# A four-layer decoder trunk on one core: tail steps of the out projection given priority over weight splits, and keys split half by half on one engine, then on the other

## The chip, the cores and the metric

The kernel runs on one core of a Trainium2 chip. The metric is the device time of one execution in microseconds (us), lower is better. The core has a TensorE (PE in the profile, with its weight loads as PEld), a VectorE (DVE), a ScalarE (ACT), a GpSimd (POOL) and a SyncE (SP) that issues most DMAs here. Each engine takes its own instructions in the order in which the program puts them, and engines wait for one another through semaphores.

## The reference

The reference is a decoder trunk in float32: batch 1, 256 tokens, model width 1024, four layers. Each layer is `h = h + mixer(rms_norm(h))`, then `h = h + mlp(rms_norm(h))`.

```python
for i in range(4):
    a = rms_norm(h, attn_norm_g[i])
    y = [diff_attention, moba_attention, swa_sink_attention][i % 3](a, ...)   # 0, 1, 2, 0
    h = h + y
    a = rms_norm(h, mlp_norm_g[i])
    h = h + (jnp.maximum(a @ w_up, 0) ** 2) @ w_down      # 1024 -> 4096 -> 1024
return rms_norm(h, final_norm_g)
```

(The middle line is shortened here: the mixers take their own weights.) Layers 0 and 3 are differential attention (8 heads, two softmaxes of 64 wide queries and keys each, one subtracted from the other), layer 1 is block-sparse attention with 16 heads, which for 256 tokens is one block, layer 2 is sliding-window attention with 16 query heads, 2 key heads and sinks. All are causal and rotate the first quarter of each head. Every mixer ends in an out projection, 1024 by 1024, and it is the end of this projection, and the splitting of keys ahead of the scores, that the change concerns.

## The kernel before, in words

**Precision.** Every large product is made of split operands. A float32 value x is kept as a high part, rounded to the form fp32r that the matmuls take, and a low part, x minus the high part. A product is the sum of three matmuls: high by high, high by low, low by high. `mm3` (L269 to L273) issues the three; `block_step` (L604 to L606) does the same with two matmuls, one of 512 columns (weight high by both halves of the activation) and one of 256 (weight low by activation high).

**Weights.** All weights stream from memory in pieces of 1 MiB, 128 partitions by 2048. `fetch` puts a piece into one of four `raw` buffers by a DMA on SP (L66). `stage` (L68 to L82) splits it in two halves of 1024 columns: ACT copies to `whi` (L80), DVE subtracts to `wlo` (L81), into three buffers each. `take` (L86 to L93) hands the next split piece to its user, and before it does so it fetches up to five pieces ahead and splits up to two pieces ahead. So the instructions of a split stand in the program where a piece further back is taken, and in the program's order they stand ahead of the work on the piece that was just taken.

**Order.** The kernel is written in a language with a scheduler: it orders each engine's instructions by priority and by when it believes their inputs to be ready. Without anything said the priority is the order of the program. `tc.high_priority()` puts the instructions issued under it ahead of all others that could be scheduled at the same point. PE's instructions are scheduled in the same way, so their order also depends on when the scheduler believes their inputs to be there.

**The residual stream.** h is held transposed in four tiles `hT[j]` of 128 by 512; each holds two column blocks of the model width, so d = 0..7 counts the eight blocks of 128, each of 256 tokens. `into` (L614 to L626) adds one block of a projection's result: DVE adds it to hT (L624). Then `norm_part` (L222 to L229) makes the operand of the next projection: ACT writes the high part of h times the gain (`hg`, L228), DVE the low part (L229). After each second block `norm_sum` (L231 to L243) squares it on ACT (L233) and DVE adds up the squares (L238, L242). The scale of the norm itself is applied later.

**The out projection** of layers 0, 2 and 3 is `out_proj_all` (L629 to L644). It holds four PSUM banks, two blocks d in each. It takes four weight pieces (g = 0..3), and for each piece runs d = 0..7 with two `mm3` each (tile `p_d`). With the last piece, g = 3, each block is complete after its six matmuls, and `into(n, d, p, None, True)` follows at once (L644). The `take()` of g = 3 has just put the split of a piece two further on into the program. After the last block comes `up_proj`: 16 groups, each with a piece of weights and two banks `p_up`; the first group goes through k, the eight blocks of `hg`, in the outer loop, so its first matmul (L605) needs `hg` of block 0 alone. Layer 1 uses `out_proj`, which the diff doesn't touch.

**The keys.** The attention of layers 0, 1 and 3 goes through four groups of queries and keys each, layer 2 has one group of keys. DVE and ACT scale and rotate the projected q and k, PE transposes them (tile `p_qk`, L461), and `put_q` and `put_k` split the transposed tile out of PSUM. For keys the two heads of a pair are in partitions 0 to 63 and 64 to 127 of one PSUM bank, and `put_k` (L474 to L478) writes each into its own columns of `kpadh` (high, ACT, L477) and `kpadl` (low, DVE, L478); the rest of these tiles is zero. `scores` then calls `mm3`, for each of two blocks of queries: its first matmul (L271) and its third (L273) need `kpadh`, its second (L272) needs `kpadl` (tile `p_s`). Between the matmuls of the scores PE has those of the next input projection (tile `p_in`, L296).

Of the kernel before, what the change touches and what calls it, by code (L numbers as in the profile page):

```python
# [24 lines left out]
HD = 64  # L25
# [9 lines left out]
def f(ap):  # L35
    return ap.bitcast(F32)
# [3 lines left out]
def trunk(ctx: ExitStack, tc: tile.TileContext, xT, gains, lams, swa_row, fng, weights, out):  # L40
# [8 lines left out]
    def bank(tag, name):  # L49
        return ps.tile([P, 512], F32, tag=tag, name=name, bufs=4)  # L50
# [35 lines left out]
    def take():  # L86
        i = used[0]
        used[0] += 1
        while len(fetched) < min(weights.shape[0], i + FAR + 1):
            fetch()  # L90
        while len(staged) < min(weights.shape[0], i + LOOK + 1):
            stage()
        return staged[i]  # L93

    def r3(n):
        return lambda t: t.rearrange("p (a b) -> p a b", a=n)
# [120 lines left out]
    def new_norm(gain):  # L217
        n = Normed()
        n.gain, n.both, n.acc = gain, [], None
        return n  # L220

    def norm_part(n, d):  # L222

        j, b = d // 2, d % 2
        if b == 0:
            n.both.append(sb.tile([P, 2, 2, S], F32R, tag=f"hg{j}", name=f"hg{j}", bufs=1))
        both, h, g = n.both[j][:, b], hT[j][:, S * b:S * b + S], n.gain[:, d:d + 1]
        A.activation(both[:, 0], h, AF.Copy, scale=g)  # L228
        V.scalar_tensor_tensor(both[:, 1], h, g, f(both[:, 0]), op0=OP.mult, op1=OP.subtract)  # L229

    def norm_sum(n, j):  # L231
        sq = sb.tile([P, 512], F32, tag="relu", name="sq")
        A.activation(sq, hT[j], AF.Square)  # L233
        if j == 0:
            n.acc = sq
        else:
            acc = sb.tile([P, 512], F32, tag="u", name="acc2")
            V.tensor_tensor(acc, n.acc, sq, op=OP.add)  # L238
            n.acc = acc
        if j == 3:  # L240
            acc = sb.tile([P, S], F32, tag="rowx", name="acc3", bufs=1)
            V.tensor_tensor(acc, n.acc[:, :S], n.acc[:, S:], op=OP.add)  # L242
            n.acc = acc  # L243
# [25 lines left out]
    def mm3(out, lh, ll, rh, rl, start, stop, **kw):  # L269

        T.matmul(out, lh, rh, start=start, stop=False, **kw)  # L271
        T.matmul(out, lh, rl, start=False, stop=False, **kw)  # L272
        T.matmul(out, ll, rh, start=False, stop=stop, **kw)  # L273
# [198 lines left out]
        return q  # L472

    def put_k(k, p, n):  # L474
        for h in range(2):
            s = slice(HD * h, HD * h + HD)
            A.activation(k[0][s, :n, h, :], p[s], AF.Copy)  # L477
            V.tensor_tensor(k[1][s, :n, h, :], p[s], f(k[0][s, :n, h, :]), op=OP.subtract)  # L478

    def mixer_layer(i, n):  # L480
# [4 lines left out]
        if mixer == 2:  # L485
# [8 lines left out]
            for t in range(NT):  # L494
                V.scalar_tensor_tensor(kv[:, t, :], p[t], r[:, t:t + 1], rest[:, :256],
                                       op0=OP.mult, op1=OP.add)
            rope(kv[:, :, 0:P].rearrange("p t (s e) -> p t s e", e=HD), 2)
            put_k(kpad, turn(lambda b, t: kv[:, t, 0:P], 1), 1)
            kT = [x[:, 0] for x in kpad]
            first, second = [], []  # L500
# [26 lines left out]
        else:  # L527
# [4 lines left out]
            def QK(c):  # L532

                qs[c] = put_q(turn(lambda j, t: qk[c][:, t, P * j:P * j + P], 2))
                put_k(kpad, turn(lambda j, t: qk[c][:, t, P * (2 + j):P * (2 + j) + P], 2), 2)
# [72 lines left out]
    def joined(out, p):  # L608

        cross = sb.tile([P, S], F32, tag="cross", name="cross")  # L610
        A.activation(cross, p[:, S:], AF.Copy)  # L611
        V.tensor_tensor(out, p[:, :S], cross, op=OP.add)  # L612

    def into(n, d, p, row, whole=False):  # L614

        j, b = d // 2, d % 2
        h = hT[j][:, S * b:S * b + S]
        y = p
        if not whole:
            y = sb.tile([P, S], F32, tag="y", name="y")  # L620
            joined(y, p)
        if row is not None:
            V.tensor_tensor(y, y, row, op=OP.mult)
        V.tensor_tensor(h, y, h, op=OP.add)  # L624
        norm_part(n, d)
        if b:  # L626
            norm_sum(n, j)

    def out_proj_all(parts, n, rest):  # L629

        banks = [bank("acc", f"p_d{j}") for j in range(4)]
        for g in range(4):
            hi, lo = (r3(2)(x) for x in take())
            for d in range(8):
                if (g, d) == (2, 4):
                    rest()
                p = banks[d // 2][:, S * (d % 2):S * (d % 2) + S]
                w = slice(P * d, P * d + P)
                for a in range(2):
                    x = parts[2 * g + a]  # L640
                    mm3(p, hi[:, a, w], lo[:, a, w], x[:, 0], x[:, 1], g + a + d % 2 == 0, g + a == 4,
                        skip_group_check=True)
                if g == 3:
                    into(n, d, p, None, True)  # L644

    def out_proj(parts, n, rest):

# [134 lines left out]
    n = new_norm(gv[:, 0, 0, :])  # L782
# [5 lines left out]
    for i in range(DEPTH):  # L788
        parts, rest = mixer_layer(i, n)
        n = new_norm(gv[:, 1, i, :])  # L790
        (out_proj if i % 3 == 1 else out_proj_all)(parts, n, rest)
        held = {}

# [21 lines left out]
        if i + 1 < DEPTH:  # L815
            n = new_norm(gv[:, 0, i + 1, :])
# [81 lines left out]
```

## Time and profile before

| | |
|---|---|
| Time, median of 3 runs | 1148.51 us (1148.4 to 1148.52) |
| Time of the profiled execution | 1148.08 us |
| Its span in the profile | 1146.0 us |
| Granted TensorE clock, mean | 0.998 of full speed |
| PEld busy | 86% of the span |
| DVE busy | 72% |
| ACT busy | 58% |
| Memory traffic | 198.66 MB, mean 173 GB/s |

The span goes from the first to the last instruction that the profiler saw; the time of the execution has 2.08 us more around it. Rows of the timeline begin with the start and the duration in us, then engine, line, operation, what is written from what, and shape; several equal instructions in a row are drawn together (x2). In brackets stands how long the engine had been idle before, and what ended it. A row of the waits reads: who waited, for whom, us in total, times, longest. Ends of matmuls are modelled and overlap the next one's start.

### The profile page before, as it was taken

The page shows a single profiled execution, that of the slowest core. Times are in us where ns is not written, and L with a number is a line of the kernel's source. Part 1 is how long each engine was busy: PE and PEld are TensorE (multiplying, and loading weights), DVE is VectorE, ACT ScalarE, POOL GpSimd, SP SyncE. Part 2 cuts the span into 40 slices and gives each one's busy share as a digit, 9 for nine tenths or more (in the row PEclk, how much of TensorE's full clock was granted, in tenths as well). Part 3 has the DMA queues.
Part 4 walks back from the last instruction along what each step waited for, and adds up shares of the span by engine and source line. Part 5 has one row for each costly group of instructions (what it writes and reads, how often), then busy time and mean ns, then how long its engine had stood idle before and what let it go on. Part 6 is the DMA issues. An engine that isn't in the chain of part 4 may idle for free.

```text
span 1146.0 us, 17054 instructions
## 1 busy us (share of the span) xinstructions
PE 1135.6 (99%) x6560; PEld 988.2 (86%) x6560; DVE 827.8 (72%) x1608; ACT 660.0 (58%) x1207; POOL 11.4 (1%) x39
## 2 busy tenths in 40 slices
PE   9999999999999999999999999999999999999997
PEld 7789888888887888888899898888888889888886
DVE  8978977656676698766569887775567788777454
ACT  6866656544476675554446756554447676665342
POOL 1000000000000000000000000000000000000000
PEclk9999999999999999999999999999999999999999
DMA  8543465555543355555563346555554444554551
GB/s 330 195 147 119 167 198 193 198 194 184 184 147 133 125 184 188 190 203 191 185 208 111 111 148 214 190 184 185 187 195 136 148 143 160 191 198 169 184 184 37
DMA packets 30609, 198.66 MB, mean 173 GB/s; under 512 B 3521, under 2 KB 5185, under 8 KB 7361
## 3 DMA queue, kind: packets, MB, share of 16 engines
q1 hardware_dynamic: 30240, 197.06, 50.2%
q8 instruction: 51, 0.84, 0.3%
q10 hardware_dynamic: 288, 0.52, 0.1%
q14 instruction: 30, 0.24, 0.1%
HBM read 196.52 MB, written 1.05 MB: 172 GB/s over the span
## 4 chain that ended last, share of the span: by engine, by line
PE 95%; DVE 2%; DMA 1%; ACT 1%; issue 0%; SPq 0%; DVEq 0%; ACTq 0%
PE p_up L605 20%; PE p_in L296 18%; PE p_down L605 15%; PE p_up L606 11%; PE p_down L606 8%; PE p_last L272 3%; PE p_last L271 3%; PE p_last L273 3%; PE p_d L272 2%; PE p_d L273 2%; PE p_d L271 2%; DMA raw<-in_weights 1%; PE p_t L354 1%; PE p_s L271 1%; PE p_qk L461 1%; PE p_av L436 1%
## 5 line engine op out<-in xcount | busy, mean ns | idle before, releaser
L81 DVE TENSOR_TENSOR wlo<-raw,whi 128x1024 fp32r<-128x1024 f32 (+1 forms) x374 | 447.2, 1209 | 204.1 <-ACT whi L80 203.3
L80 ACT ACTIVATE whi<-raw 128x1024 fp32r<-128x1024 f32 (+1 forms) x374 | 384.3, 1046 | 216.4 <-issue 111.1
L605 PE MATMUL p_up<-hg,whi 128*128 128x512 f32 x1024 | 356.7, 393 | 0.5 <-DVE hg L229 0.2
L606 PE MATMUL p_up<-hg,wlo 128*128 128x256 f32 x1024 | 285.5, 280 | 0.0
L605 PE MATMUL p_down<-uu,whi 128*128 128x512 f32 x768 | 266.4, 391 | 0.0
L605 PEld LDWEIGHTS p_up<-hg,whi 128*128 128x128 f32 x1024 | 191.4, 187 | 42.8 <-DVE hg L229 0.7
L606 PE MATMUL p_down<-uu,wlo 128*128 128x256 f32 x768 | 215.0, 280 | 0.0
L296 PE MATMUL p_in<-whi,hg 128*128 128x512 f32 (+1 forms) x736 | 211.6, 371 | 0.0
L606 PEld LDWEIGHTS p_up<-hg,wlo 128*128 128x128 f32 x1024 | 193.5, 189 | 0.5
L605 PEld LDWEIGHTS p_down<-uu,whi 128*128 128x128 f32 x768 | 143.6, 187 | 31.5
L296 PEld LDWEIGHTS p_in<-whi,hg 128*128 128x128 f32 x736 | 132.2, 189 | 23.3 <-DVE hg L229 0.8
L606 PEld LDWEIGHTS p_down<-uu,wlo 128*128 128x128 f32 x768 | 145.2, 189 | 0.0
L296 PE MATMUL p_in<-wlo,hg 128*128 128x512 f32 (+1 forms) x368 | 130.4, 369 | 0.1
L680 ACT ACTIVATE uu<-u 128x512 fp32r<-128x512 f32 x64 | 40.5, 633 | 71.1 <-DVE u L678 71.1
L296 PEld LDWEIGHTS p_in<-wlo,hg 128*128 128x128 f32 x368 | 68.8, 189 | 12.3 <-DVE wlo L81 1.4
L611 ACT ACTIVATE cross<-p_up 128x256 f32<-128x256 f32 x128 | 47.9, 374 | 39.3 <-PE p_up L606 33.8
L228 ACT ACTIVATE hg<-hT,gn 128x256 fp32r<-128x256 f32 x64 | 31.6, 502 | 65.5 <-DVE hT L624 65.3
L339 ACT ACTIVATE e<-ns,nm 128x128 f32<-128x128 f32 (+1 forms) x128 | 56.8, 446 | 11.6 <-DVE nm L336 11.2
L681 DVE TENSOR_TENSOR uu<-u,uu 128x512 fp32r<-128x512 f32 x64 | 44.2, 691 | 21.4 <-ACT uu L680 21.4
L272 PE MATMUL p_d<-oo,whi 128*128 128x256 f32 x192 | 55.3, 288 | 0.0
L271 PE MATMUL p_d<-oo,whi 128*128 128x256 f32 x192 | 55.2, 288 | 0.0
L612 DVE TENSOR_TENSOR relu<-p_up,cross 128x256 f32<-128x256 f32 x128 | 53.6, 419 | 1.5 <-ACT cross L611 1.5
(182 smaller groups left out, 1247.2 us busy)
## 6 DMA issues: line engine op xcount, KB each, us to landing
raw<-in_weights SPq DMA_DIRECT2D x181, 1024.0 KB, 4.9
raw<-in_weights SPq DMA_DIRECT2D x8, 256.0 KB, 4.6
raw<-in_weights SPq DMA_DIRECT2D x4, 512.0 KB, 6.8
hT<-in_xT SPq DMA_DIRECT2D x8, 128.0 KB, 4.4
bias<-in_swa_row SPq DMA_DIRECT2D x1, 512.0 KB, 4.6
grow<-in_fng SPq DMA_DIRECT2D x1, 512.0 KB, 3.7
out<-res SPq DMA_DIRECT2D x4, 128.0 KB, 2.1
out<-res ACTq DMA_DIRECT2D x2, 256.0 KB, 2.2
```

The lines of the kernel that those rows point to most:

```text
L80: A.activation(hi[:, s], raw[:, s], AF.Copy)
L81: V.tensor_tensor(lo[:, s], raw[:, s], f(hi[:, s]), op=OP.subtract)
L271: T.matmul(out, lh, rh, start=start, stop=False, **kw)
L272: T.matmul(out, lh, rl, start=False, stop=False, **kw)
L273: T.matmul(out, ll, rh, start=False, stop=stop, **kw)
L296: T.matmul(out[t], n.both[k // 2][:, k % 2, x, P * t:P * t + P], r3(kb)(parts[k // kb][w])[:, k % kb, :], start=fresh, stop=k == 7 and x + ...
L339: A.activation(e[:, s], ns[:, s], AF.Exp, bias=nm[:, t:t + 1], scale=-1.0, accum_out=l[:, t:t + 1])
L605: T.matmul(r3(2)(p), hi, x, start=start, stop=False, skip_group_check=True)
L606: T.matmul(p[:, :S], lo, x[:, 0], start=False, stop=stop, skip_group_check=True)
L611: A.activation(cross, p[:, S:], AF.Copy)
L612: V.tensor_tensor(out, p[:, :S], cross, op=OP.add)
L681: V.tensor_tensor(both[:, :, 1], r3(2)(u), f(both[:, :, 0]), op=OP.subtract)
```

## The change

Two edits. `put_k` runs its two ACT copies first and then its two DVE subtractions, where it alternated between the engines before. In `out_proj_all` the call of `into` for a finished block is put under `tc.high_priority()`, so that its steps (L624, L228, L229, L233, L238, L242) are scheduled ahead of the weight splits (L80, L81) that stand before them in the program. Both kernels have the same instructions on every engine; their order differs on PE, DVE and ACT. On SP and POOL it is the same. After the change lines 479 to 643 have numbers higher by one, and later ones by two.

```diff
     def put_k(k, p, n):
-        for h in range(2):
-            s = slice(HD * h, HD * h + HD)
+        rows = [slice(HD * h, HD * h + HD) for h in range(2)]
+        for h, s in enumerate(rows):
             A.activation(k[0][s, :n, h, :], p[s], AF.Copy)
+        for h, s in enumerate(rows):
             V.tensor_tensor(k[1][s, :n, h, :], p[s], f(k[0][s, :n, h, :]), op=OP.subtract)
...
                 if g == 3:
-                    into(n, d, p, None, True)
+                    with tc.high_priority():
+                        into(n, d, p, None, True)
```

## The prediction

> **What bounds the kernel now.** I read the head of the page first, then the chain that ended last, then PE's own row of the waits, and only then the timelines of the places that the diff touches.
>
> ```profile
> span 1146.0 us, 17054 instructions
> ...
> PE 1135.6 (99%) x6560; PEld 988.2 (86%) x6560; DVE 827.8 (72%) x1608; ACT 660.0 (58%) x1207; POOL 11.4 (1%) x39
> ...
> PE 95%; DVE 2%; DMA 1%; ACT 1%; issue 0%; SPq 0%; DVEq 0%; ACTq 0%
> ```
>
> PE is busy 99% of the span and 95% of the chain. A kernel like this can only become faster where PE stands still. The view of waits gives all of these places:
>
> ```profile
> PE p_warm L133 <- POOL ones L124: 1.0, 1, 1.0
> PE p_qk L461 <- DVE qk L309: 0.7, 1, 0.7
> PE p_s L271 <- issue: 0.6, 1, 0.6
> PE p_up L605 <- DVE hg L229: 0.2, 1, 0.2
> ```
>
> That is 2.5 us, and only the last two lines touch the diff. The ends of matmuls are modelled, though, so a short stall hides inside a longer "busy" matmul. I therefore measure stalls by the distance from one start to the next. Nothing in the diff adds or removes an instruction; the same instructions stand in another order on PE, DVE and ACT, and SP's queue keeps its order. So the whole effect is stalls of PE that go or come.
>
> **Part 1, the end of the out projection (layers 0, 2 and 3; layer 1 uses another function).** In layer 0, DVE does this:
>
> ```profile
> 116.10 0.42 DVE L624 TENSOR_TENSOR hT<-p_d,hT 128x256 f32<-128x256 f32 x1 [2.12 <-PE p_d L273]
> 116.44 2.35 DVE L81 TENSOR_TENSOR wlo<-raw,whi 128x1024 fp32r<-128x1024 f32 x2
> 118.71 0.48 DVE L229 SCALAR_TENSOR_TENSOR hg<-hT,gn,hg 128x256 fp32r<-128x256 f32 x1
> 119.11 1.08 DVE L624 TENSOR_TENSOR hT<-p_d,hT 128x256 f32<-128x256 f32 x3
> ```
> ```profile
> 117.17 0.49 ACT L228 ACTIVATE hg<-hT,gn 128x256 fp32r<-128x256 f32 x1
> ```
> ```profile
> 118.83 0.28 PE L273 MATMUL p_d<-oo,wlo 128*128 128x256 f32 x1
> 119.25 0.50 PE L605 MATMUL p_up<-hg,whi 128*128 128x512 f32 x1
> 119.58 0.28 PE L606 MATMUL p_up<-hg,wlo 128*128 128x256 f32 x1
> 119.70 0.39 PE L605 MATMUL p_up<-hg,whi 128*128 128x512 f32 x1
> 119.93 0.28 PE L606 MATMUL p_up<-hg,wlo 128*128 128x256 f32 x1
> ```
>
> The high half of hg for block 0 is ready at 117.66, but its low half waits behind two weight splits (2.35 us) until 118.71. It ends at 119.19, and the up projection starts at 119.25. A 256-column matmul is followed after 0.12 us (119.58 to 119.70), a 512-column one after 0.23 (119.70 to 119.93). So 119.25 - 118.83 - 0.12 = 0.30 is lost, and 119.58 - 119.25 - 0.23 = 0.10 more behind it: 0.40 us. The other two layers show the same picture:
>
> ```profile
> 666.61 0.28 PE L273 MATMUL p_d<-oo,wlo 128*128 128x256 f32 x1
> 667.11 0.47 PE L605 MATMUL p_up<-hg,whi 128*128 128x512 f32 x1 [0.22 <-DVE hg L229]
> 667.41 0.28 PE L606 MATMUL p_up<-hg,wlo 128*128 128x256 f32 x1
> ```
> ```profile
> 957.72 0.28 PE L273 MATMUL p_d<-oo,wlo 128*128 128x256 f32 x1
> 958.12 0.50 PE L605 MATMUL p_up<-hg,whi 128*128 128x512 f32 x1
> 958.46 0.28 PE L606 MATMUL p_up<-hg,wlo 128*128 128x256 f32 x1
> ```
>
> Layer 2 loses 0.38 + 0.07, layer 3 loses 0.28 + 0.11. Together with layer 0 this is 0.40 + 0.45 + 0.39 = **1.24 us**, which is all that the first edit can win here.
>
> Does it win it? In the order of the changed kernel DVE does hT of block 0, only the first half of that split, and then hT and hg of the blocks as they come; the second half waits until nearly all blocks are through. By the durations above (1.18 for half the split, 0.33 from one hT to the next, 0.40 for an hg), hT of blocks 1, 2 and 4 are done at 118.6 and the hg of blocks 0 and 1 at 119.25 and 119.65. PE, in turn, has 18 matmuls of other blocks put ahead of p_up, so p_up comes at about 120.27, 0.6 us after its inputs. I take the whole 1.24 as gained. The bounds are 0 (another step of the row ends late in its place) and 1.24; the margin of 0.6 us puts it near the upper end.
>
> What is late next is the postponed second half of the split. DVE has the same work in the same stretch, so it does this one at about 124.2 to 125.4 instead of 117.6 to 118.8. PE needs it at step 4 of the second up group: from 120.27, sixteen steps of 0.12 + 0.23 = 0.35 us, six matmuls of the last block (0.7) and four more steps make 128.0. It has 2.6 us in hand. The raw buffer that it frees goes to a load on SP's queue:
>
> ```profile
> 118.82 0.33 SPq L66 DMA_DIRECT2D raw<-in_weights  x1
> ```
> ```profile
> raw<-in_weights SPq DMA_DIRECT2D x181, 1024.0 KB, 4.9
> ```
> ```profile
> 138.79 1.06 ACT L80 ACTIVATE whi<-raw 128x1024 fp32r<-128x1024 f32 x1 [1.33 <-PE p_up L605]
> ```
>
> The load is issued at 118.82, as the pair of splits ends. In the changed kernel it goes out at about 125.4 and lands 4.9 us later, at 130.3, and ACT reads that piece at 138.79. Nothing waits for it on SP but later loads of the same kind. I cost the postponed split at nothing; DVE's slack covers it, and without that cover each layer would pay up to the half split, 1.2 us.
>
> **Part 2, the keys.** Before, ACT splits keys of half 0, DVE subtracts them, then ACT does half 1:
>
> ```profile
> 317.95 0.58 ACT L477 ACTIVATE kpadh<-p_qk 64x512 fp32r<-64x512 f32 x1
> 319.41 0.59 ACT L477 ACTIVATE kpadh<-p_qk 64x512 fp32r<-64x512 f32 x1 [0.88 <-DVE kpadl L478]
> ```
> ```profile
> 318.70 0.67 DVE L478 TENSOR_TENSOR kpadl<-p_qk,kpadh 64x512 fp32r<-64x512 f32 x1
> ```
> ```profile
>   DVE kpadl L478: 8.5, 11
> ```
>
> The second ACT step starts 0.04 us after DVE's ends (318.70 + 0.67 = 319.37); the view of line 477 counts 11 such waits, 8.5 us on ACT. Both read the same PSUM bank, and the program has them take turns. Page "PSUM — Partial Sum Buffer" of the Trainium skill, section "PSUM bank collisions raise a hardware error", says that two engines may use one bank at once if their partition quadrants differ; the halves here lie in different quadrants. No run here shows such an overlap: by that rule the turns are the program's alone and new places for the instructions would gain nothing in the keys, which makes the sum of part 1 alone, 1147.3. In the changed order ACT does both halves in a row, without a wait for DVE, and half 1 ends about 1 us earlier (317.95 + 0.48 + 0.59 = 319.0 against 320.0). ACT's 8.5 us are themselves worth nothing, since ACT is 58% busy. What counts is when PE's first score matmul can start:
>
> ```profile
> 34.50 0.61 PE L296 MATMUL p_in<-whi,hg 128*128 128x512 f32 x2
> 35.72 0.59 PE L271 MATMUL p_s<-kpadh,qhl 128*128 128x256 f32 x2 [0.60 <-issue]
> ```
> ```profile
> 319.84 0.39 PE L296 MATMUL p_in<-wlo,hg 128*128 128x512 f32 x1
> 320.15 0.59 PE L271 MATMUL p_s<-kpadh,qhl 128*128 128x256 f32 x2
> ```
> ```profile
> 32.52 0.59 ACT L477 ACTIVATE kpadh<-p_qk 64x512 fp32r<-64x512 f32 x1
> 32.99 2.01 ACT L80 ACTIVATE whi<-raw 128x1024 fp32r<-128x1024 f32 x2
> 35.03 0.59 ACT L477 ACTIVATE kpadh<-p_qk 64x512 fp32r<-64x512 f32 x1
> ```
>
> At 35.72 PE has stood still for 35.72 - 34.50 - 2 x 0.23 = 0.76 us: two weight splits lie between the two key steps. That is the one large stall. At 320.15 it is 320.15 - 319.84 - 0.23 = 0.08. But the scheduler, which sees the keys ready earlier, also moves the first score matmuls ahead of 4 to 10 others in PE's order, at 11 places. In layer 0 they move ahead of 8 p_in: PE is there at 34.96 - 8 x 0.23 = 33.12, the keys are there at 32.52 + 0.48 + 0.59 = 33.59 and 0.10 later a matmul can start (as at 35.62 to 35.72), so PE waits 0.57 and gains 0.19. At 320.15 they move ahead of 5: arrival 318.92, keys 319.02 + 0.10, a wait of 0.20, so 0.12 is lost. The other places lie between no wait at all and a loss like this one. I take a loss of 0.05 at each of the ten, 0.5 us; the ends are a gain of 0.08 each (every wait goes, -0.8) and a loss of 0.2 each (+2.0).
>
> **The sum.** -1.24 - 0.19 + 0.5 = -0.9 us. The profiled execution took 1148.08 for a span of 1146.0, 2.08 outside it. After: span 1145.1, execution 1147.2. The median of the runs before is 1148.51, 0.43 above the profiled one, so the forecast is 1148.51 - 0.9 = **1147.6**. With the ends of the keys, and with 0 to 1.24 for the tails, this case alone reaches from 1146.3 to 1150.3 by its extremes, and I hold 1147.0 to 1148.2 for its core. A measurement of this kernel can tell about 0.2%, 2.3 us, from no change, so this counts as the same.
>
> **Rivals.**
> - *Every touched stall goes*: tails 1.24, the whole 0.76, and the waits of about 0.08 at ten places, 0.8: -2.8, 1145.7. For it: the keys are indeed ready 1 us earlier. Against it: the matmuls move by about as much.
> - *The score waits eat the tails' gain*: a loss of 0.13 at 11 places is 1.4, and the time is 1148.5. For it: the 0.12 worked out at 318.92.
> - *Slower, by the scores.* PE takes its matmuls in order, so a score matmul that is placed too early holds all the p_in behind it, as the 0.60 at 35.72 shows. (Page "TensorE: Matmul & The Clock Gate" of the Trainium skill, section on the 64-deep queue and the weight pull-ahead, says the same; this row agrees.) If half 1 of the keys isn't earlier, since ACT comes late to the pair, PE waits the whole moved distance, 4 x 0.23 = 0.92 or more. It decides from a mean loss of 1.43 / 11 = 0.13 us a place, and at 0.4 a place the time is 1148.51 - 1.43 + 4.4 = 1151.5. Against it: the ACT row at 317.95 starts on time now.
> - *The postponed split starves the up projection*: 1.2 us in three layers, 3.6 less the 1.4 gained, 1150.7. Against it: 2.6 us in hand.
> - *The change doesn't do what it says*: the scheduler leaves the splits where they are, and the first half of the split does stay ahead of hg. Then only the keys change: 1148.8.
>
> **Chances.** Forecast 0.48; every stall goes 0.14; waits eat the gain 0.16; slower by scores 0.10; starved 0.07; not done 0.05. Faster by over 0.2% (under 1146.2): most of the first rival and none of the forecast, 0.12. Slower by over 0.2% (over 1150.8): the slower half of the two slow rivals and what I have overlooked, 0.11. The same: 0.77. The range leaves out about 0.08 below and 0.10 above: 1146.0 to 1150.4.
>
> **What would show it.** Right: p_up starts 0.12 us after the last p_d ahead of it at all three tails; the second ACT key step follows the first without a wait for DVE; the first score of layer 0 has its wait cut from 0.76 to some 0.6. Wrong: PE waits for wlo in the second up group; waits of p_s on ACT kpadh that sum to over 2 us; a PE busy sum that differs from 1135.6 for a reason other than stalls.

## The result and the profile after

| Kernel | Median | Runs | Against before |
|---|---|---|---|
| before | 1148.51 us | 8 | |
| after | 1152.02 us | 8 (1151.35 to 1152.43) | 1.0029 (95%: 1.0020 to 1.0038) |

The change makes the kernel slower by 3.5 us, 0.3%. The forecast was 1147.6 us, and the time is above the upper end of the range, 1150.4. The profiled execution of after took 1152.43 us for a span of 1150.5, so the two profiles lie 4.5 us apart where the medians lie 3.5 apart.

The head of the page and the chain of after:

```profile
span 1150.5 us, 17080 instructions
...
PE 1138.9 (99%) x6560; PEld 987.9 (86%) x6560; DVE 828.3 (72%) x1608; ACT 660.6 (57%) x1207; POOL 11.4 (1%) x39
...
PE 94%; ACT 3%; DMA 1%; DVE 1%; issue 0%; SPq 0%; DVEq 0%; ACTq 0%
```

The numbers of matmuls and of DVE and ACT instructions are the same as before; the 26 instructions more in the first line are waits for semaphores, which don't count as busy. PE is busy 3.3 us longer with the same matmuls, and ACT has 3% of the chain where it had 1%. The view of PE's waits (who, for whom, us in total, times, longest) says where ACT came in:

```profile
PE p_s L271 <- ACT kpadh L477: 1.1, 6, 0.2
PE p_warm L133 <- POOL ones L124: 1.0, 1, 1.0
PE p_qk L461 <- DVE qk L309: 0.6, 1, 0.6
PE p_in L296 <- DVE wlo L81: 0.5, 1, 0.5
PE p_s L271 <- issue: 0.5, 1, 0.5
```

The first line is new: six first score matmuls wait for the ACT half of the key split. The wait of the up projection for `hg`, 0.2 us before, is gone. The same two things appear in the timelines.

**The tails.** DVE in layer 0 of after has one half of the split ahead of the `hg` steps, and the other behind them:

```profile
117.66 1.22 DVE L81 TENSOR_TENSOR wlo<-raw,whi 128x1024 fp32r<-128x1024 f32 x1
118.81 1.26 DVE L625 TENSOR_TENSOR hT<-p_d,hT 128x256 f32<-128x256 f32 x3
119.99 0.87 DVE L229 SCALAR_TENSOR_TENSOR hg<-hT,gn,hg 128x256 fp32r<-128x256 f32 x2
...
125.36 1.22 DVE L81 TENSOR_TENSOR wlo<-raw,whi 128x1024 fp32r<-128x1024 f32 x1
```

PE at the tails of layers 2 and 3 of after:

```profile
670.66 0.28 PE L273 MATMUL p_d<-oo,wlo 128*128 128x256 f32 x1
670.78 0.40 PE L606 MATMUL p_up<-hg,whi 128*128 128x512 f32 x1
671.01 0.28 PE L607 MATMUL p_up<-hg,wlo 128*128 128x256 f32 x1
```
```profile
962.41 0.28 PE L273 MATMUL p_d<-oo,wlo 128*128 128x256 f32 x1
962.53 0.40 PE L606 MATMUL p_up<-hg,whi 128*128 128x512 f32 x1
962.77 0.28 PE L607 MATMUL p_up<-hg,wlo 128*128 128x256 f32 x1
```

The up projection starts 0.12 us after the last out projection matmul ahead of it, where it started 0.50 and 0.40 after it before, and its second matmul follows 0.23 and 0.24 later. Layer 0 shows the same:

```profile
121.49 0.28 PE L273 MATMUL p_d<-oo,wlo 128*128 128x256 f32 x1
121.61 0.40 PE L606 MATMUL p_up<-hg,whi 128*128 128x512 f32 x1
```

The stalls of the tails are gone.

**The keys.** ACT and PE at the first keys of layer 1 of after:

```profile
318.86 1.20 ACT L477 ACTIVATE kpadh<-p_qk 64x512 fp32r<-64x512 f32 x2
```
```profile
319.63 0.40 PE L296 MATMUL p_in<-whi,hg 128*128 128x512 f32 x1
320.21 0.58 PE L271 MATMUL p_s<-kpadh,qhl 128*128 128x256 f32 x2 [0.18 <-ACT kpadh L477]
```

ACT doesn't wait for DVE between its two copies any more. But PE comes to the first score at 319.63 + 0.23 = 319.86 and starts it at 320.21: it stands still for 0.35 us where it lost 0.08 before. (The view of waits shows only 0.18 of it, since the matmul ahead is drawn as busy until 320.03.)

**The last up projection.** The matmuls of layer 3's up projection from 985 to 1045 us, grouped by line, before and then after (the columns are count, busy us and mean ns):

```profile
L605 PE MATMUL p_up<-hg,whi 128*128 128x512 f32 x174 | 60.4, 391 | 0.0
```
```profile
L606 PE MATMUL p_up<-hg,whi 128*128 128x512 f32 x171 | 60.5, 399 | 0.0
```

In 60 us PE starts 171 matmuls of 512 columns instead of 174, without any wait. At one place of both timelines, for two pairs of matmuls:

```profile
1000.12 0.39 PE L605 MATMUL p_up<-hg,whi 128*128 128x512 f32 x1
1000.36 0.28 PE L606 MATMUL p_up<-hg,wlo 128*128 128x256 f32 x1
1000.47 0.39 PE L605 MATMUL p_up<-hg,whi 128*128 128x512 f32 x1
1000.70 0.28 PE L606 MATMUL p_up<-hg,wlo 128*128 128x256 f32 x1
1000.82 0.39 PE L605 MATMUL p_up<-hg,whi 128*128 128x512 f32 x1
```
```profile
1000.08 0.40 PE L606 MATMUL p_up<-hg,whi 128*128 128x512 f32 x1
1000.32 0.28 PE L607 MATMUL p_up<-hg,wlo 128*128 128x256 f32 x1
1000.43 0.40 PE L606 MATMUL p_up<-hg,whi 128*128 128x512 f32 x1
1000.66 0.28 PE L607 MATMUL p_up<-hg,wlo 128*128 128x256 f32 x1
1000.78 0.40 PE L606 MATMUL p_up<-hg,whi 128*128 128x512 f32 x1
1001.02 0.28 PE L607 MATMUL p_up<-hg,wlo 128*128 128x256 f32 x1
1001.14 0.40 PE L606 MATMUL p_up<-hg,whi 128*128 128x512 f32 x1
```

Before, a pair takes 0.35 us each time. After, three pairs take 1001.14 - 1000.08 = 1.06, which is 0.353 each. Three matmuls fewer of 174, 1.7%, make 1.5 us over the 87 us that this goes on. **This was not in the prediction at all.**

**The start.** One part of the 4.5 us is seen in this execution alone: at 18.09 in after, and at 18.11 in a second profile of the same kernel.

```profile
18.09 0.73 PE L296 MATMUL p_in<-whi,hg 128*128 128x512 f32 x2
19.35 0.50 PE L296 MATMUL p_in<-wlo,hg 128*128 128x512 f32 x1 [0.53 <-DVE wlo L81]
```
```profile
18.11 0.63 PE L296 MATMUL p_in<-whi,hg 128*128 128x512 f32 x2
18.73 0.51 PE L296 MATMUL p_in<-wlo,hg 128*128 128x512 f32 x1
```

At 19.9 after is 0.76 us behind before, the second profile at the same matmul only 0.14. So this is a difference between executions, and may account for some of the gap between 4.5 and 3.5.

### The profile page after: what moved, and what is told of

Same layout as the page of the kernel before. It is cut to its first block, busy times and chain, and to the rows that moved or that the text cites. A ratio compares the mean times of both kernels' runs of the same rounds, so it can differ in the third digit from the quotient of the medians.

```text
span 1150.5 us, 17080 instructions
## 1 busy us (share of the span) xinstructions
PE 1138.9 (99%) x6560; PEld 987.9 (86%) x6560; DVE 828.3 (72%) x1608; ACT 660.6 (57%) x1207; POOL 11.4 (1%) x39
## 4 chain that ended last, share of the span: by engine, by line
PE 94%; ACT 3%; DMA 1%; DVE 1%; issue 0%; SPq 0%; DVEq 0%; ACTq 0%
PE p_up L606 21%; PE p_in L296 17%; PE p_down L606 15%; PE p_up L607 11%; PE p_down L607 8%; PE p_last L273 3%; PE p_last L272 3%; PE p_last L271 3%; PE p_d L271 2%; PE p_d L272 2%; PE p_d L273 2%; PE p_s L271 1%; PE p_t L354 1%; PE p_av L436 1%; DMA raw<-in_weights 1%; PE p_s L272 1%
## 5 line engine op out<-in xcount | busy, mean ns | idle before, releaser
L81 DVE TENSOR_TENSOR wlo<-raw,whi 128x1024 fp32r<-128x1024 f32 (+1 forms) x374 | 447.0, 1209 | 212.2 <-ACT whi L80 211.0
L80 ACT ACTIVATE whi<-raw 128x1024 fp32r<-128x1024 f32 (+1 forms) x374 | 384.1, 1045 | 215.2 <-issue 111.1
L339 ACT ACTIVATE e<-ns,nm 128x256 f32<-128x256 f32 (+1 forms) x128 | 56.8, 446 | 27.4 <-DVE nm L336 27.2
L228 ACT ACTIVATE hg<-hT,gn 128x256 fp32r<-128x256 f32 x64 | 31.4, 503 | 61.2 <-DVE hT L625 61.2
L273 PE MATMUL p_d<-oo,wlo 128*128 128x256 f32 x192 | 53.8, 284 | 0.0
```

Of the source, the lines that this page charges most:

```text
L80: A.activation(hi[:, s], raw[:, s], AF.Copy)
L81: V.tensor_tensor(lo[:, s], raw[:, s], f(hi[:, s]), op=OP.subtract)
L339: A.activation(e[:, s], ns[:, s], AF.Exp, bias=nm[:, t:t + 1], scale=-1.0, accum_out=l[:, t:t + 1])
```

## The experiments

Two theories at first. **A**: the keys cost the time, since the score matmuls move further forward than the keys do. **B**: the tail's priority does, by what it postpones. The first three kernels take the change apart.

**Keys alone.** The diff of `put_k` only.

> Only the key split of the change; the tail as before. Theory A (score matmuls moved ahead of keys that are not much earlier): in the changed kernel PE stands still some 0.3 us at each of about ten first scores where it stood 0.1 before, 2.0 us in all, so 1148.5 + 2.0 = 1150.5 here, or up to 1153.2 if the slower cadence of the last up projection and the longer start come with the keys. Theory B (the tail's priority starves or disturbs the up projections): 1148.5 to 1149.0 here.

Measured: 1151.59 us, ratio 1.0028 (1.0017 to 1.0038), against 1148.57 for before, measured beside it. +3.0 us, so the keys carry nearly all of the loss. The last up projection runs as before, 175 matmuls in those 60 us, so its slower cadence does not come with the keys.

**Tail alone.** The diff of `out_proj_all` only.

> Only the priority at the end of the out projection; keys as before. Theory A: the 1.24 us of the three tails are won, 1147.3. Theory B: slower than before, about 1151, with the up projection of layer 3 at 236 ns between matmuls of 512 columns where it had 230.

Measured: 1148.76 us, ratio 1.0003 (0.9994 to 1.0013). Neither theory has it: the gain of 1.24 doesn't show, and neither does a loss of 2.5. The stalls of the three tails are gone here too, and layer 3 has the slow cadence:

```profile
L605 PE MATMUL p_up<-hg,whi 128*128 128x512 f32 x171 | 60.5, 399 | 0.0
```

**Keys with later scores.** The key split, and the priority of the scores lowered by 28 places of the program's order:

```diff
+        at = tc.cur_priority
+        tc.cur_priority = at + 28
         for p, t, n in ((p0, 0, P), (p1, 1, S)):
             ...
             mm3(o, qh[:, a], ql[:, a], kh[:, :, :n], kl[:, :, :n], True, True)
+        tc.cur_priority = at + 6
```

In PE's order the first score then stands at, or within two matmuls of, its old place in eight of the twelve cases of layers 0, 1 and 3.

> The key split of the change, and the score matmuls given a later place in the program's priority, so that at eight of the eleven places PE's first score stands where it stood before. Theory A: the waits at these eight places go, about 8 x 0.28 = 2.2 us less than the key split alone, so 1148.3 to 1149. Theory B, and any theory in which the keys harm by something else: no different from the key split alone.

Measured: 1149.15 us, ratio 1.0005 (0.9996 to 1.0014), just over the 1149 of theory A. The key split is the same, ACT's two copies still stand in a row, and 2.4 of the 3.0 us are gone. At the first keys of layer 1 PE no longer waits:

```profile
320.15 0.39 PE L296 MATMUL p_in<-wlo,hg 128*128 128x512 f32 x1
320.37 0.28 PE L271 MATMUL p_s<-kpadh,qhl 128*128 128x256 f32 x1
```

So most of the harm is done by the place of the scores in PE's order, not by the key split as such: theory A holds for the keys. 0.6 us stays that the first scores don't explain.

**After, once more.** A second profile of the changed kernel.

> The changed kernel once more, for a second profile. If the longer start (0.76 us by 19.9) and the slower cadence in the up projection of layer 3 (236 ns, 1.7 us) belong to the kernel, both are there again; if they are chance, one or both are gone, and the rest (score waits of about 0.35 us, tails shorter by 0.4) stays.

Measured: 1151.88 us, span 1149.9. The longer start is gone, so it differs from execution to execution. The slow cadence is there again (170 matmuls of 512 columns in the 60 us from 985), so at this place it goes with the kernel. The waits of the scores are the same to 0.02 us.

From here the tail needed a theory of its own. **C**: each tail wins its 0.4 us, and layer 3 gives back 1.5 because its up projection falls into a slower cadence of PE. **D**: the tails win nothing.

**Tails of layers 0 and 2 only.** `early`, a new argument of `out_proj_all`, is true in these two (the call is left out here).

```diff
                 if g == 3:
-                    into(n, d, p, None, True)
+                    if early:
+                        with tc.high_priority():
+                            into(n, d, p, None, True)
+                    else:
+                        into(n, d, p, None, True)
```

> The priority at the tails of layers 0 and 2 only; layer 3 and the keys as before. Theory C (each tail wins its 0.4 us, and layer 3 gives 1.6 back because its up projection then runs at 353 us per thousand pairs of matmuls instead of 347): layer 3 is as before, with 230 and 117 ns between its matmuls, and the time is 1148.55 - 0.8 = 1147.7. Theory D (the tail's edit gains nothing anywhere, or all tails lose later): 1148.5 or more.

Measured: 1147.97 us against 1148.70, ratio 0.9994 (0.9985 to 1.0002). The median has the forecast size, -0.7, though the interval reaches just over 1. The last up projection has 174 matmuls again. In the profile layers 0 and 2 win 0.32 and 0.35 us, of the 0.40 and 0.45 that their stalls were.

**Tail of layer 3 only.** The same with the condition the other way round.

> The priority at the tail of layer 3 only. Theory C: 0.39 won at its tail, 1.6 lost in the up projection behind it at 236 ns per 512 columns, so +1.2: 1149.7. Theory D: within 0.3 of before, 1148.5; or, if the slow cadence in layer 3 came from what happens in layers 0 and 2, 230 ns and 1148.1.

Measured: 1149.94 us, ratio 1.0010 (1.0001 to 1.0019), +1.2. In the profile it is 0.16 us behind the kernel before where layer 3 begins, and 1.40 behind at the end, with the slow cadence between (171 matmuls in the 60 us).

The two together make the kernel with all three tails: -0.7 + 1.2 = +0.5 against +0.2 measured. The same edit wins in two layers and loses in the third.

**All tails, and two matmuls more in layer 3.** Layers 0 and 2 have a mean of two matmuls behind the first group of their up projection (`mean_row`, L261); layer 3 has transposes there. With the tails alone, layer 0 too begins its up projection at the slow cadence, and leaves it at this mean. Its matmuls from 124 to 132 us and from 135 to 143, ahead of the mean and behind it:

```profile
L605 PE MATMUL p_up<-hg,whi 128*128 128x512 f32 x24 | 8.5, 399 | 0.0
```
```profile
L605 PE MATMUL p_up<-hg,whi 128*128 128x512 f32 x24 | 8.4, 391 | 0.0
```

(The mean of one is 399 ns at the slow cadence and 391 at the fast one.) Here layer 3 gets such a mean behind its transposes, and nobody reads it:

```diff
                     for t in range(NT):
                         A.activation(held["res"][t][:, S * j:S * j + S], p[:, S * t:S * t + S], AF.Copy)
+                mean_row(n)
```

> All three tails have the priority, the keys are as before, and in layer 3 two matmuls of 128 columns more (a mean that nobody reads) stand behind the transposes of the second group of the up projection, as layers 0 and 2 have them there. If the slow cadence is a phase of PE that a disturbance can end, as those two end it in layers 0 and 2, layer 3 goes on at 230 and 117 ns and the time is 1148.55 - 1.24 + 0.4 = 1147.7. If it comes from other traffic in layer 3 (DVE, ACT or DMA beside it), the cadence stays at 236 and the time is some 1149.2.

Measured: 1148.23 us, ratio 0.9995 (0.9986 to 1.0004), 0.5 less than the tails alone. The cadence is that of before in sum, with a third division between the two matmuls of a pair:

```profile
L605 PE MATMUL p_up<-hg,whi 128*128 128x512 f32 x174 | 60.4, 394 | 0.0
L606 PE MATMUL p_up<-hg,wlo 128*128 128x256 f32 x174 | 48.2, 277 | 0.0
```

So the slow cadence looks like a state of PE that outlives its beginning. A load on DVE, ACT or DMA doesn't explain it: these do the same work beside it, but for one small DVE instruction.

**All tails, and two steps of the first group in another order.** In before, layer 3 also begins its up projection slowly, and changes at a place where two matmuls of 256 columns stand in a row:

```profile
965.07 0.28 PE L606 MATMUL p_up<-hg,wlo 128*128 128x256 f32 x1
965.19 0.40 PE L605 MATMUL p_up<-hg,whi 128*128 128x512 f32 x1
965.43 0.40 PE L606 MATMUL p_up<-hg,wlo 128*128 128x256 f32 x2
965.66 0.40 PE L605 MATMUL p_up<-hg,whi 128*128 128x512 f32 x1
```

The scheduler put them so; with the tail's priority the group is regular. The next kernel puts two such places back by hand:

```diff
+                if g == 0 and k in (5, 6):
+                    x = n.both[k // 2][:, k % 2]
+                    T.matmul(r3(2)(ps_up[b]), hi[:, k, w], x, start=False, stop=False, skip_group_check=True)
+                    if b == 1:
+                        for c in range(2):
+                            T.matmul(ps_up[c][:, :S], lo[:, k, P * c:P * c + P], x[:, 0], start=False, stop=False,
+                                     skip_group_check=True)
+                else:
+                    block_step(ps_up[b], hi[:, k, w], lo[:, k, w], n.both[k // 2][:, k % 2], k == 0, k == 7)
```

> All three tails have the priority, keys as before; in the first group of each up projection two steps (k = 5 and 6) issue their four matmuls as 512, 512, 256, 256 columns instead of 512, 256, 512, 256. The kernel before has two such places there, by its scheduler's choice, and leaves the slow cadence at them; the tail's priority removes them. If that is what keeps layer 3 slow, it runs at 230 ns per 512 columns again (174 matmuls in the 60 us from 985) and the time is 1148.6 - 1.24 = 1147.4, or some tenths less since layers 0 and 2 leave the slow cadence earlier too. If the slow cadence hangs on something else, layer 3 stays at 236 and the time at 1148.8.

Measured: 1147.81 us against 1148.59, ratio 0.9994 (0.9984 to 1.0003), with 174 matmuls in the 60 us and the 277 ns form of the fast cadence. The 1.2 us that layer 3 lost with the tails alone are a gain of 0.3 in this profile. But it didn't go as put: the two places don't end the slow cadence. The three pairs that begin at 966.02, behind both places, still take 1.06 us, and the fast cadence sets in behind the transposes of the second group, which did not end it with the tails alone.

```profile
966.02 0.40 PE L605 MATMUL p_up<-hg,whi 128*128 128x512 f32 x1
...
967.08 0.40 PE L605 MATMUL p_up<-hg,whi 128*128 128x512 f32 x1
```

So irregular places may change the state, and in which state PE comes out seems to hang on what went before. In the last up projection it goes with PE's order: all four profiles with the order of the tails alone are slow there, all six with the order of before fast.

But the order does not decide it everywhere. Layer 1 ends its out projection with 32 pairs of 512 and 256 columns (tile `p_e`). The kernel with all three tails and the one with those of layers 0 and 2 have the same order on PE, DVE and ACT up to layer 3's tail, and yet the first is fast at this place and the second slow:

```profile
L605 PE MATMUL p_e<-oo,whi 128*128 128x512 f32 x32 | 11.1, 391 | 0.0
```
```profile
L605 PE MATMUL p_e<-oo,whi 128*128 128x512 f32 x32 | 11.4, 399 | 0.0
```

Before is fast here, and each of the six profiles with the key split is slow. None of these runs shows what chooses the state, and that stays open.

**Both copies on all partitions.** Back to the keys: the copies start 0.61 us apart, which I had put at 0.48. In the profile of after, ACT at the first keys of layer 0:

```profile
33.25 1.20 ACT L477 ACTIVATE kpadh<-p_qk 64x512 fp32r<-64x512 f32 x2
34.48 2.01 ACT L80 ACTIVATE whi<-raw 128x1024 fp32r<-128x1024 f32 x2
```

The pair ends at 34.45, and the split behind it starts after that. In before, a split started at 32.99 while the first copy ran until 33.11. The first copy takes partitions 0 to 63, the second 64 to 127. The kernel lets both take all 128. That leaves out the zero halves of the high keys, so its scores are sums over two heads; the instructions and their order are those of the key split alone:

```diff
         for h, s in enumerate(rows):
-            A.activation(k[0][s, :n, h, :], p[s], AF.Copy)
+            A.activation(k[0][:, :n, h, :], p, AF.Copy)
```

> The key split alone, but both ACT copies take all 128 partitions, not 64 each, so the zero halves of the high keys are overwritten and the scores are sums over both heads. If the second copy's start at 0.61 instead of 0.48 us comes from the half partition range (64 to 127), it starts 0.48 after the first now, PE's waits at ten first scores get shorter by 0.13, and the time is 1151.6 - 1.4 = 1150.2. If it comes from reading the same bank or writing the same tile twice in a row, the spacing stays at 0.61 and the time at 1151.6.

Measured: 1150.13 us, ratio 1.0013 (1.0004 to 1.0021), 1.46 less than the key split alone, with the same order on PE, DVE and ACT. The pair of copies:

```profile
318.65 1.09 ACT L477 ACTIVATE kpadh<-p_qk 128x512 fp32r<-128x512 f32 x2
```

The pair takes 1.09 instead of 1.20 us, so the second begins before the first has ended (0.59 + 0.59 = 1.18). Bank and tile are the same as with the key split alone, so it is the range of partitions.

**Both faults taken out.** The change with later scores and no priority in layer 3, that is the edits of the third and fifth kernel together.

> Both edits of the change, with the two faults found taken out: the score matmuls a little later in the program's priority, and no priority at the tail of layer 3. If the parts add up (the keys with late scores cost 0.6, the tails of layers 0 and 2 win 0.7), the time is that of before, 1148.6 + 0.6 - 0.7 = 1148.5, and the 3.5 us of the change are accounted for. If something in the change that was not found still costs, it is 1149.5 or more.

Measured: 1148.99 us against 1148.48, ratio 1.0003 (0.9994 to 1.0012). It is 0.5 over what the parts add up to, which is within the interval; 3.0 of the change's 3.5 us are gone. Three kernels have medians below that of before: the tails of layers 0 and 2 alone (-0.7), all tails with the two steps reordered (-0.8), and all tails with the mean added (-0.5). All three intervals end just above 1, so none is shown to be faster.

## Why the prediction was wrong

The stall of PE ahead of the first score of each block of keys, by starts as above (start of the score, less that of the matmul ahead, less the usual distance behind such a matmul), in us; the four of layer 2 are the same throughout and left out:

| | layer 0 | layer 1 | layer 3 | sum |
|---|---|---|---|---|
| before | 0.76, 0, 0.01, 0.20 | 0.08, 0.05, 0.04, 0.09 | 0.08, 0.01, 0, 0.20 | 1.52 |
| after | 0.68, 0, 0.27, 0.34 | 0.35, 0.36, 0.13, 0.36 | 0.35, 0.31, 0.28, 0.33 | 3.76 |
| keys, all partitions | 0.52, 0, 0.17, 0.23 | 0.14, 0.26, 0.01, 0.26 | 0.16, 0.20, 0.18, 0.24 | 2.37 |
| keys, later scores | 0.68, 0, 0, 0.34 | 0, 0, 0, 0 | 0, 0, 0, 0.33 | 1.35 |

**The step that failed is the loss at the score matmuls.** The prediction took "a loss of 0.05 at each of the ten, 0.5 us". The table has twelve places, where the prediction counted eleven; those other than the first lose 3.08 - 0.76 = 2.3 us, 0.21 each. That is a little past the upper end of 0.2 each, 2.0 us in all, with which it had bounded them. The mechanism, a score matmul that comes too early and holds all behind it, stood there as the rival "slower, by the scores"; but the condition given there, that ACT comes late to the pair, did not hold. The step that failed is the size of the term, for two reasons.

- *The copies.* 0.48 from one to the next was taken from a copy on partitions 0 to 63 with an instruction on all 128 behind it. It is 0.61, so half 1 is 0.86 us earlier (320.00 before; 320.06 after, where everything at this place is 0.92 later) and not 1.0. At the place that was worked out this makes the forecast wait of 0.20 into 0.33, and 0.35 was measured. All partitions take 1.4 us off the sum in the table and 1.46 off the time.
- *The choice between the ends.* One place had been worked out at a loss of 0.12, and the others were put at less without being worked out. Most were worse: at seven of the eleven the scheduler moved the scores by five matmuls of 512 columns, 1.15 us, while the keys came about 0.86 earlier. That makes a loss of 0.29, and 0.26 to 0.31 was measured. At the one place with a move of four, 0.92 us, it was 0.09.

**"So the whole effect is stalls of PE that go or come"** was wrong too. The tail's own term of 1.24 us was right: all three stalls went, p_up started 0.12 after the matmul ahead, and the postponed split kept nobody waiting. But in layer 3 the same matmuls went on at 0.353 us a pair where they had taken 0.347, and the 1.5 us that this costs are more than the tails won. Before has both cadences (0.355 a pair from 963.77 to 965.19, 0.347 from 967.07 on), but no row of it shows that a new order can keep PE in the slow one.

**The first keys** gained 0.08, not 0.19, for the same 0.13 us between the copies.

**What the sum would have been**: -1.24 - 0.08 + 2.3 + 1.5 = +2.5 us, of the 4.5 in the profiles. 0.76 more is the start. The remaining 1.2 has no single place. 0.7 of it lies in layer 1, which takes 1.68 us longer while the table explains 0.94. The key split alone, and with all partitions, have the same 0.7 there; with later scores 0.55 is left, and 0.3 even with the tails of layers 0 and 2 alone, where the keys are as before. Half of the 0.7, 0.37 us, is the slow cadence at the end of layer 1's out projection (tiles `p_d` and `p_e`), which all of these kernels have. The rest is not shown.

**The other rivals.** The postponed split never starved the up projection: no wait of `p_up` is in the list of after. The score matmuls that wait hold the p_in behind them, as the rival had it. That two engines could read different quadrants of one bank at once, as the page "PSUM — Partial Sum Buffer" of the Trainium skill says in the section "PSUM bank collisions raise a hardware error", remains untried: here too DVE's first subtraction starts only after both copies (320.10 after 320.06).

## What to carry to other kernels

When an edit makes an input earlier and a scheduler orders the engine that bounds the kernel, look at how far its consumers move, in time, and set that against how much earlier the input really is; an order that is too eager costs more than the wait it removed. Price such an input by a row of the very same form, partitions included. And where a kernel runs at 99% of one engine, count that engine's instructions per stretch in both profiles, since a cadence can change where nothing was edited.

## What the runs showed of the hardware

- **A copy on partitions 64 to 127 overlaps neither neighbour.** Two ACT copies in a row on partitions 0 to 63 and 64 to 127 took 1.20 us together, which is more than twice 0.59; on all 128 partitions 1.09, overlapping by 0.1. The instruction behind the second also started only after its end (34.48 after 34.45).
- **PE has more than one steady cadence for the same stream.** Pairs of 512 and 256 columns at a granted clock of 0.998 to 0.999 ran at 0.347 or at 0.353 us, for the whole rest of an up projection. There, two matmuls of 256 columns more, or another order of a few, went with the fast one (174 matmuls of 512 columns in 60 us, where it was 171); in layer 1 the same order gave either (391 and 399 ns for a matmul of 512 columns). The Trainium skill, page "TensorE: Matmul & The Clock Gate", section "Back-to-back issue gap", gives N / 2.4 + 2.5 ns for an isolated matmul of N columns (about 216 for 512; an estimate by it is 109 for 256 and 325 a pair), and about 131 ns for 512 columns in a sustained stream. Here both cadences are slower than either figure.
